# The feed-forward input products, turned: weight columns stand in the array and the tokens move

## The chip, the cores and the metric

The kernel runs on one core of one Trainium2 chip. The metric is the device time of one execution in microseconds. A core has five engines with instruction queues of their own: TensorE (PE, matmuls; PEld is its loading of the operand that stands in the array), VectorE (DVE), ScalarE (ACT), GpSimd (POOL) and SyncE (SP, which here issues DMAs). They wait for one another by semaphores, and each does its instructions in the order of its queue. Matmuls write to PSUM; VectorE and ScalarE read it.

## The reference

A decoder trunk of two residual layers over 256 tokens of 2048 channels, conditioned on a vector c. Layer 0 mixes by a gated recurrence and softmax attention, layer 1 by gated linear attention; each layer ends with a SwiGLU feed-forward network (FFN) of 5632 hidden channels. All numbers are float32.

```
D_MODEL = 2048; SEQ = 256; DEPTH = 2; D_FF = 5632

def swiglu(h, w_in, w_out):
    a, u = jnp.split(h @ w_in, 2, axis=-1)
    return (jax.nn.silu(a) * u) @ w_out

for layer in range(DEPTH):
    mod = silu_c @ mod_w[layer] + mod_b[layer]
    sh1, sc1, g1, sh2, sc2, g2 = jnp.split(mod, 6, axis=-1)
    h = modulate(rms_norm(x, norm_mix_gain[layer]), sh1, sc1)
    y = hgrn2_fox_mixer(h, ...) if layer % 2 == 0 else gla_mixer(h, ...)
    x = x + g1[:, None, :] * y
    h = modulate(rms_norm(x, norm_ffn_gain[layer]), sh2, sc2)
    x = x + g2[:, None, :] * swiglu(h, ffn_w_in[layer], ffn_w_out[layer])
```

`ffn_w_in` has 2048 rows and 11264 columns in each layer: 5632 for `a`, 5632 for `u`.

## The kernel before

All large products are done with split numbers: an operand is rounded to TensorE's float32r (its high part, `hi`), what is left over is the low part (`lo`), and a product is the sum of three matmuls, high by high, high by low and low by high. Activations are split when they are made: a buffer `hT` or `ct` of the pool `hpool` holds [128 channels, 2 parts, 4 k tiles, 256 tokens]. Weights come as float32 and are split on the way.

The products are one long stream. `add` appends a `Product`, 512 columns of a weight matrix by all of its rows, to a list of pieces. A piece is half of a 1 MB transfer, 1024 weight columns per partition: two k tiles of 128 rows by 512 columns. `drive` walks through the pieces. For piece i it issues what the other parts of the network owe at this place (`run_jobs`), splits the pieces up to i + 2 (`split`: ScalarE copies to `hi`, L166, and VectorE subtracts to `lo`, L168), requests the raw weights of some pieces more on SP's queue (`load`, L159), and multiplies (`multiply`). Raw tiles have 3 buffers, `hi` and `lo` 4 each. In `multiply` the activations stand and the weights move: for each k tile and each of two token tiles, three matmuls (L189 to L191) with 512 moving columns, into an accumulator `acc` of [128 tokens, 2 token tiles, 512 columns], two banks of PSUM. The pool `pp` has two such accumulators, `pm` four single banks for all else.

An FFN input product `F{layer}_{n}` has 256 columns of `a` and the 256 of `u` that belong to them; there are 22 in a layer. Its `done_ffn` has ScalarE take the Silu of the first half out of PSUM (L1141), VectorE multiply by the second (L1142), and two pieces later, as a job, `turn`: TensorE transposes the four 128x128 blocks against an identity (L1148), ScalarE copies the high part to a `ct` buffer (L370) and VectorE subtracts for the low part (L371). The 22 products go in four groups (`FFN_GROUPS`); after a group's products, and one more of the next group, come its four output products `G{layer}_{group}_{nb}`, which use the group's `ct` buffers as standing operand.

Between the pieces run the modulation columns: `mod_block` fetches 1 MB of `mod_w` on GpSimd's queue (L103) and VectorE multiplies and sums it (L108). `run_mod` issues them at a rate, `need_mod` issues those that are left of a part when it is wanted: for the FFN's gate in layer 0 that is at product 4 (`begin_row`). The first product of a layer, `F{layer}_0`, comes straight after a norm, and its first four pieces go one token tile after the other (`by_tile`). `narrow_product` (L274) is another form: the weights of the low-rank gate stand, padded to 128 columns, and 256 tokens move.

The instructions of one engine are put in order by a scheduler that uses the order of the code and its own estimate of times.

Of the kernel before, what the change touches and what calls it, by code (L numbers as in the profile page):

```python
# [7 lines left out]
F32 = mybir.dt.float32  # L8
# [3 lines left out]
ALU = mybir.AluOpType  # L12
# [17 lines left out]
# pieces of the products within which the mixers' steps are to be issued  # L30
# [9 lines left out]
# columns of the packed per-partition parameters  # L40
# [10 lines left out]
class Job:  # L51
    """Steps of arithmetic to be issued between the pieces of the streamed products, before a given piece."""
# [6 lines left out]
class Product:  # L59
    def __init__(self, name, w, act, done, before=None, rate=0.0):  # L60
        self.name, self.w, self.act, self.done, self.before, self.rate = name, w, act, done, before, rate
        self.ps = None
        self.first = self.last = False


def build(tc, ctx, a, out):
# [74 lines left out]
    def add(name, w, act, done, before=None, rate=0.0, first=False, last=False):  # L141
        p = Product(name, w, act, done, before, rate)
        p.first, p.last = first, last
        pieces.extend((p, k) for k in range(2 * len(w)))
# [31 lines left out]
    def multiply(i, tiles=(0, 1)):  # L176
        p, k = pieces[i]
        if p.ps is None:
            p.ps = env["pp"].tile([P, 2, 512], F32, tag="pp", name=f"acc_{p.name}")
        hi, lo = splits[i]  # L180
        last = 4 * len(p.w) - 1
        for kk in range(2):
            kt = k * 2 + kk
            w_hi = hi[:, kk * 512:(kk + 1) * 512]
            w_lo = lo[:, kk * 512:(kk + 1) * 512]
            for t in tiles:
                a_hi, a_lo = p.act(kt, t)
                o = p.ps[:, t, :]
                nc.tensor.matmul(o, a_hi, w_hi, start=(kt == 0), stop=False)  # L189
                nc.tensor.matmul(o, a_hi, w_lo, start=False, stop=False)  # L190
                nc.tensor.matmul(o, a_lo, w_hi, start=False, stop=(kt == last))  # L191

# [86 lines left out]
    def rsqrt(dst, ss, n, width, name):  # L279
        """(ss / n + eps) ** -0.5 with one Newton step."""  # L280
        m = small.tile([P, width], F32, tag=f"rs_m{width}", name=f"rsm_{name}")
        u = small.tile([P, width], F32, tag=f"rs_u{width}", name=f"rsu_{name}")
        nc.vector.tensor_scalar(m, ss, 1.0 / n, EPS, ALU.mult, ALU.add)
        nc.scalar.activation(u, m, AF.Ln)
        nc.scalar.activation(dst, u, AF.Exp, scale=-0.5)
        nc.vector.scalar_tensor_tensor(u, dst, -0.5, dst, ALU.mult, ALU.mult)
        nc.vector.tensor_tensor(u, u, m, ALU.mult)
        nc.vector.scalar_tensor_tensor(dst, u, 1.5, dst, ALU.add, ALU.mult)

    def softplus_neg_abs(dst, z):  # L290
        """ln(1 + exp(-|z|))"""
# [39 lines left out]
    def norm_tile(t):  # L331
        """Normalize, modulate, transpose and split one token tile of x."""
# [26 lines left out]
    def ct_pair(key, n):  # L359
        """Pair n of the split, transposed activations called key: two k tiles of a four-tile buffer."""  # L360
# [19 lines left out]
    def gate_line(l, part):  # L380
        """The gate as a line in DRAM."""
# [35 lines left out]
    class Recurrence:  # L417
        """Both token tiles of one head. q, k: [P, tile, d]; lf: [P, tile, 2, d] (split); v: [P, tile, dv]."""
# [63 lines left out]
        def scores(self, t, levels, dst):  # L482
            """dst(n) -> PSUM [P, 64] of level n"""
# [8 lines left out]
        def cross(self, diagonal):  # L492
            """Scores between the token tiles, and with diagonal those of each token with itself."""
# [13 lines left out]
        def pick(self, n, ts, src):  # L507
            """scatter the compact scores of level n; src: [P, len(ts), 64]"""
# [133 lines left out]
    def fox_gates():  # L642
        """-log f, split, [token, head] per token tile; and -F in columns."""
# [207 lines left out]
    def gla_scores(u):  # L851
# [35 lines left out]
    def gla_output(u):  # L887
        """(steps that need v, steps that need the gate too)"""
# [217 lines left out]
    def begin_out(l, src):  # L1106
        """The old x and the gate row take buffers that the mixer's activations leave."""
# [26 lines left out]

    def done_ffn(l, i):
        def done(ps):
            s = env["pool"].tile([P, 2, 256], F32, tag="fs", name=f"fs{l}_{i}")
            if i == FFN_GROUPS[-1][1] - 1:
                silu_then_exp_ln(s, ps[:, :, :256])
            else:  # L1140
                nc.scalar.activation(s, ps[:, :, :256], AF.Silu)  # L1141
            nc.vector.tensor_tensor(s, s, ps[:, :, 256:], ALU.mult)  # L1142

            def turn():
# [4 lines left out]
                gi = [n for n, (b, e) in enumerate(FFN_GROUPS) if b <= i < e][0]  # L1149
# [36 lines left out]
    def now_act(kt, t):  # L1186
        return env["act"](kt, t)
# [4 lines left out]
    def add_ffn(l, rate):  # L1192
        w1, w2 = a["ffn_w_in"], a["ffn_w_out"]
# [89 lines left out]
def _tiles(w, groups):  # L1283
    """w (K, N) and lists of 512 columns -> (chunk, quad, 128, 4 * 512)."""
# [10 lines left out]
def _layout(i):  # L1295
# [35 lines left out]
    groups = [np.concatenate([r(n * 256, n * 256 + 256), DFF + r(n * 256, n * 256 + 256)]) for n in range(DFF // 256)]  # L1331
    arrays["ffn_w_in"] = np.stack([_tiles(i["ffn_w_in"][l], groups) for l in range(2)])
# [22 lines left out]
```

## Time and profile before

| | |
|---|---|
| median of 3 runs | 2524.02 us (2519.18, 2524.24, 2524.02) |
| profiled execution, its own time (the span on the page) | 2515.9 us |
| TensorE busy | 2450.4 us, 11316 matmuls |
| weight loads of TensorE (PEld) | 2025.2 us |
| VectorE busy | 1771.8 us |
| ScalarE busy | 1160.2 us |
| moved by DMA | 647.49 MB, mean 257 GB/s |

The page and the answers of the trace have engines, source lines, tile names, shapes (partitions x elements), counts, busy time and mean time of one instruction, and behind a bar the idle time ahead of them with what ended it. `acc_F` are the accumulators of the FFN's input products, `acc_G` those of its output products, `acc_C` those of layer 1's mixer. In a timeline the first number is the start in us from the span's start, the second how long. A matmul's length there is from its start to its last result; they are pipelined, and the distance of two starts is what one adds to the time.

### The profile page before, as it was taken

What the parts mean: (1) busy time and instruction counts of PE and PEld (TensorE: products, weight loads), DVE (VectorE), ACT (ScalarE), POOL (GpSimd) and SP (SyncE); (2) the same over time, 40 slices, a digit from 0 to 9 for tenths busy, and PEclk for the clock granted to TensorE, in tenths of its full rate; (3) what the DMA queues carried; (4) which work ended last, traced back from release to release, by engine and by line L of the source; (5) the groups of instructions that cost most, each with busy time, mean ns of one, the idle gap of its engine ahead of it and who ended that gap; (6) DMA issues with size and microseconds to landing.
All of it is one profiled execution on the core that took longest, in us unless ns stands there. A gap on an engine that the chain in (4) does not pass through costs nothing.

```text
span 2515.9 us, 28838 instructions
## 1 busy us (share of the span) xinstructions
PE 2450.4 (97%) x11316; PEld 2025.2 (80%) x11316; DVE 1771.8 (70%) x1975; ACT 1160.2 (46%) x1600; POOL 89.4 (4%) x174
## 2 busy tenths in 40 slices
PE   5899999999999999999999999999999999999999
PEld 3678887887888888888888888888788888888887
DVE  6986887877688767766777777777676545554555
ACT  4365555545434444344345545554544344344443
POOL 0000000000000000000000000000000000000000
PEclk9999999999999999999999999999999999999999
DMA  9973767885899878777776566677477555555554
GB/s 379 422 272 140 274 257 292 340 319 216 287 349 357 317 281 293 287 277 293 287 277 226 202 243 233 242 256 283 169 296 254 191 194 184 196 188 186 199 185 149
DMA packets 93850, 647.49 MB, mean 257 GB/s; under 512 B 10417, under 2 KB 10993, under 8 KB 16401
## 3 DMA queue, kind: packets, MB, share of 16 engines
q1 hardware_dynamic: 70290, 476.59, 52.1%
q0 software_dynamic: 23424, 169.07, 18.1%
q8 instruction: 88, 1.44, 0.2%
q14 instruction: 48, 0.39, 0.0%
HBM read 641.39 MB, written 4.23 MB: 257 GB/s over the span
## 4 chain that ended last, share of the span: by engine, by line
PE 92%; DVE 6%; ACT 1%; issue 0%; DMA 0%; SPq 0%; ACTq 0%; DVEq 0%
PE acc_F L191 13%; PE acc_F L190 13%; PE acc_F L189 13%; PE acc_G L189 6%; PE acc_G L191 6%; PE acc_G L190 6%; PE acc_C L191 4%; PE acc_C L189 4%; PE acc_C L190 3%; DVE mod_s L108 3%; PE acc_B L189 2%; PE acc_B L190 2%; PE acc_B L191 2%; PE acc_O L189 2%; PE acc_O L191 2%; PE acc_O L190 2%
## 5 line engine op out<-in xcount | busy, mean ns | idle before, releaser
L168 DVE TENSOR_TENSOR lo<-raw_F,hi 128x1024 fp32r<-128x1024 f32 x352 | 429.4, 1224 | 296.9 <-ACT hi L166 296.8
L166 ACT CAST hi<-raw_F 128x1024 fp32r<-128x1024 f32 x352 | 370.5, 1053 | 478.3 <-PE acc_F L191 430.0
L191 PE MATMUL acc_F<-hi,hT_f 128*128 128x512 f32 x1408 | 551.3, 392 | 1.4 <-DVE hT_f L355 1.4
L189 PE MATMUL acc_F<-hi,hT_f 128*128 128x512 f32 x1408 | 548.4, 390 | 1.8 <-ACT hT_f L354 1.8
L190 PE MATMUL acc_F<-lo,hT_f 128*128 128x512 f32 x1408 | 548.5, 390 | 0.0
L108 DVE SCALAR_TENSOR_TENSOR mod<-mod,silu_c 128x2048 f32<-128x2048 f32 x160 | 365.4, 2285 | 11.1 <-DMA mod<-in_mod_w_dram 11.1
L168 DVE TENSOR_TENSOR lo<-raw_G,hi 128x1024 fp32r<-128x1024 f32 x176 | 214.2, 1222 | 138.3 <-ACT hi L166 138.1
L191 PEld LDWEIGHTS acc_F<-hi,hT_f 128*128 128x128 f32 x1408 | 264.4, 188 | 56.6 <-DVE hT_f L355 3.0
L189 PEld LDWEIGHTS acc_F<-hi,hT_f 128*128 128x128 f32 x1408 | 264.5, 188 | 56.1 <-ACT hT_f L354 2.2
L166 ACT CAST hi<-raw_G 128x1024 fp32r<-128x1024 f32 x176 | 185.4, 1054 | 268.6 <-PE acc_G L191 224.8
L190 PEld LDWEIGHTS acc_F<-lo,hT_f 128*128 128x128 f32 x1408 | 264.3, 188 | 55.2
L189 PE MATMUL acc_G<-hi,ct_f 128*128 128x512 f32 x704 | 273.5, 389 | 1.6 <-DVE res_G L403 1.6
L191 PE MATMUL acc_G<-hi,ct_f 128*128 128x512 f32 x704 | 274.4, 390 | 0.0
L190 PE MATMUL acc_G<-lo,ct_f 128*128 128x512 f32 x704 | 273.8, 389 | 0.0
L168 DVE TENSOR_TENSOR lo<-raw_C,hi 128x1024 fp32r<-128x1024 f32 x96 | 116.8, 1222 | 58.4 <-ACT hi L166 58.0
L189 PEld LDWEIGHTS acc_G<-hi,ct_f 128*128 128x128 f32 x704 | 132.2, 188 | 29.6 <-DVE res_G L403 2.4
L189 PE MATMUL acc_C<-hi,hT_n 128*128 128x512 f32 x384 | 154.3, 402 | 0.9 <-ACT hT_n L354 0.9
L190 PEld LDWEIGHTS acc_G<-lo,ct_f 128*128 128x128 f32 x704 | 132.2, 188 | 27.4
L191 PEld LDWEIGHTS acc_G<-hi,ct_f 128*128 128x128 f32 x704 | 132.2, 188 | 27.2
L191 PE MATMUL acc_C<-hi,hT_n 128*128 128x512 f32 x384 | 150.5, 392 | 0.7 <-DVE hT_n L355 0.7
L190 PE MATMUL acc_C<-lo,hT_n 128*128 128x512 f32 x384 | 150.9, 393 | 0.0
L166 ACT CAST hi<-raw_C 128x1024 fp32r<-128x1024 f32 x96 | 100.7, 1052 | 94.7 <-PE acc_C L191 88.4
(335 smaller groups left out, 3424.0 us busy)
## 6 DMA issues: line engine op xcount, KB each, us to landing
raw_F<-in_ffn_w_in_dram SPq DMA_DIRECT2D x176, 1024.0 KB, 4.9
mod<-in_mod_w_dram POOLq DMA_DIRECT2D x160, 1024.0 KB, 5.2
raw_G<-in_ffn_w_out_dram SPq DMA_DIRECT2D x88, 1024.0 KB, 4.9
raw_C<-in_gla_w_in_dram SPq DMA_DIRECT2D x48, 1024.0 KB, 6.0
mod_s<-in_mod_w_dram SPq DMA_DIRECT2D x32, 1024.0 KB, 10.6
raw_B<-in_ab_w_in_dram SPq DMA_DIRECT2D x32, 1024.0 KB, 5.9
raw_s<-in_start_w_dram SPq DMA_DIRECT2D x16, 1024.0 KB, 8.8
raw_A<-in_ab_w_in_dram SPq DMA_DIRECT2D x16, 1024.0 KB, 5.0
```

The costliest lines, as they stand in the source:

```text
L108: nc.vector.scalar_tensor_tensor(tile, tile, 1.0, silu_c, ALU.mult, ALU.mult, accum_out=modc[l, part][:, j:j + 1])
L166: nc.scalar.copy(out=hi, in_=w)
L168: env["lo"] = nc.vector.tensor_tensor(lo, w, hi, ALU.subtract)
L189: nc.tensor.matmul(o, a_hi, w_hi, start=(kt == 0), stop=False)
L190: nc.tensor.matmul(o, a_hi, w_lo, start=False, stop=False)
L191: nc.tensor.matmul(o, a_lo, w_hi, start=False, stop=(kt == last))
```

## The change

Products 1 to 21 of each layer's FFN are turned: the weight columns stand in the array and the tokens move, so that the result is channel-major and goes to the `ct` buffer without a transpose. Product 0 stays as it was. A turned product comes in two halves, each a `Product` of its own with 128 columns of `a` and their 128 of `u`: 256 columns by 2048 rows, two transfers of 1 MB, 4 pieces. A piece now has four k tiles of 256 columns. Its accumulator has for each of the two 128-column blocks one bank: 256 tokens by the high part of the activations, and 256 by the low part. The high part of the weights is multiplied with both in one matmul of 512 moving columns, the low part with the high part of the activations alone, 256 moving columns, into the first half of the bank. At the end the two halves of the bank are added.

```diff
-    def add(name, w, act, done, before=None, rate=0.0, first=False, last=False):
+    def add(name, w, act, done, before=None, rate=0.0, first=False, last=False, turned=False):
...
         hi, lo = splits[i]
+        if p.turned:
+            multiply_turned(p, k, hi, lo)
+            return
...
+    def multiply_turned(p, k, hi, lo):
+        for kk in range(4):
+            kt = k * 4 + kk
+            both = p.act(kt)
+            for c in range(2):
+                cs = slice(kk * 256 + c * P, kk * 256 + (c + 1) * P)
+                o = p.ps[:, c]
+                nc.tensor.matmul(o, hi[:, cs], both, start=(kt == 0), stop=False, skip_group_check=True)
+                nc.tensor.matmul(o[:, :T], lo[:, cs], both[:, 0], start=False, stop=(kt == KT - 1), skip_group_check=True)
...
-        def act(kt, t):
+        def act(kt, t=None):
             tl = tiles(kt // 4) if callable(tiles) else tiles[kt // 4]
+            if t is None:
+                return tl[:, :, kt % 4, :]
...
+    def done_ffn_turned(l, i, half):
+        def done(ps):
+            s = env["pool"].tile([P, 2, T], F32, tag="fs", name=f"fs{l}_{i}_{half}")
+            nc.scalar.copy(out=s, in_=ps[:, :, T:])
+            nc.vector.tensor_tensor(s, s, ps[:, :, :T], ALU.add)
+            if i == FFN_GROUPS[-1][1] - 1 and half == 1:
+                silu_then_exp_ln(s[:, 0], s[:, 0])
+            else:
+                nc.scalar.activation(s[:, 0], s[:, 0], AF.Silu)
+            nc.vector.tensor_tensor(s[:, 0], s[:, 0], s[:, 1], ALU.mult)
+            gi = group_of(i)
+            c, k0 = ct_pair(f"f{l}{gi}", i - FFN_GROUPS[gi][0])
+            nc.scalar.copy(out=c[:, 0, k0 + half], in_=s[:, 0])
+            nc.vector.tensor_tensor(c[:, 1, k0 + half], s[:, 0], c[:, 0, k0 + half], ALU.subtract)
+        return done
...
-                add(f"F{l}_{n}", quads(w1[l, n]), now_act, done_ffn(l, n), before, rate, n == 0)
+                if n == 0:
+                    add(f"F{l}_{n}", quads(w1[l]), now_act, done_ffn(l, n), before, rate, True)
+                else:
+                    for half in range(2):
+                        m = 2 * n + half - 2
+                        add(f"F{l}_{n}_{half}", [wt[l, m, qd] for qd in range(2)], now_act, done_ffn_turned(l, n, half),
+                            before if half == 0 else None, rate, turned=True)
...
+    w = i["ffn_w_in"].reshape(2, 2, 8, P, 2, DFF // P, P)[:, :, :, :, :, 2:]
+    arrays["ffn_w_turned"] = np.ascontiguousarray(w.transpose(0, 5, 1, 3, 2, 4, 6)).reshape(2, DFF // P - 2, 2, P, 2048)
```

The order of instructions, first on TensorE, in layer 0's product 10, where piece 233 ends and piece 234 begins. `acc_F0_10` is the product's accumulator, `hi_234` and `lo_234` the split weights of piece 234, `hT_f0_1` the second buffer of activations, `fs0_9` the gated result of product 9. Before:

```order
L191 MATMUL acc_F0_10_6857<-hi_233_6822,hT_f0_0_4669 128x512
L189 MATMUL acc_F0_10_6857<-hi_234_6851,hT_f0_1_4670 128x512
L190 MATMUL acc_F0_10_6857<-lo_234_6852,hT_f0_1_4670 128x512
L1148 MATMUL hT_F0_9_6844<-ident_74,fs0_9_6841 128x128 x4
L191 MATMUL acc_F0_10_6857<-hi_234_6851,hT_f0_1_4670 128x512
```

Now, the same piece (in the first half of product 10):

```order
L204 MATMUL acc_F0_10_0_7190<-hT_f0_1_4670,hi_233_7154 128x512
L205 MATMUL acc_F0_10_0_7190<-hT_f0_1_4670,lo_233_7155 128x256
L204 MATMUL acc_F0_10_0_7190<-hT_f0_2_4671,hi_234_7184 128x512
L205 MATMUL acc_F0_10_0_7190<-hT_f0_2_4671,lo_234_7185 128x256
L204 MATMUL acc_F0_10_0_7190<-hT_f0_2_4671,hi_234_7184 128x512
```

Matmuls of 512 and 256 columns take turns, 16 in a piece where 12 of 512 were, and the four transposes of the product ahead are gone.

Next VectorE, at the end of layer 0's FFN input: product 21 is the last, and its result is wanted by the fourth group's output products. `lo_379` to `lo_383` are splits of the output weights (piece 376 is the first of `G0_3_0`, 380 the first of `G0_3_1`), `mod1_3_6` is a modulation column, `ct_f03_1` the buffer that takes the result. Before:

```order
L1142 TENSOR_TENSOR fs0_21_9569<-fs0_21_9569,acc_F0_21_9432 128x512
L168 TENSOR_TENSOR lo_379_9600<-raw_G0_3_0_1_9465,hi_379_9599 128x1024
L168 TENSOR_TENSOR lo_380_9616<-raw_G0_3_1_0_9502,hi_380_9615 128x1024
L168 TENSOR_TENSOR lo_381_9634<-raw_G0_3_1_0_9502,hi_381_9633 128x1024
L108 SCALAR_TENSOR_TENSOR mod1_3_6_9649,modc1_3_91<-mod1_3_6_9649,silu_c_72 128x2048
L371 TENSOR_TENSOR ct_f03_1_9423<-hT_F0_21_9573,ct_f03_1_9423 128x512
```

Now:

```order
L168 TENSOR_TENSOR lo_379_10377<-raw_G0_3_0_1_10213,hi_379_10376 128x1024
L1159 TENSOR_TENSOR fs0_21_1_10349<-fs0_21_1_10349,acc_F0_21_1_10267 128x512
L168 TENSOR_TENSOR lo_380_10393<-raw_G0_3_1_0_10265,hi_380_10392 128x1024
L1164 TENSOR_TENSOR fs0_21_1_10349<-fs0_21_1_10349 128x256
L168 TENSOR_TENSOR lo_381_10411<-raw_G0_3_1_0_10265,hi_381_10410 128x1024
L108 SCALAR_TENSOR_TENSOR mod1_3_6_10426,modc1_3_91<-mod1_3_6_10426,silu_c_72 128x2048
L1168 TENSOR_TENSOR ct_f03_1_10068<-fs0_21_1_10349,ct_f03_1_10068 128x256
```

Three instructions of half 21_1, add, multiply and subtraction, stand between the splits where a multiply and a subtraction stood, and the subtraction still comes last, behind the split of piece 381 and a modulation column. On TensorE the output product that follows begins with piece 376; the first matmul that uses the high part of half 21_1 has 50 matmuls of `G0_3_0` and `G0_3_1` ahead of it, the first that uses the low part 66.

More of the change, by code (lines that the diff above doesn't have):

```diff
@@ L62, in __init__ @@
         self.ps = None
-        self.first = self.last = False
+        self.first = self.last = self.turned = False
 def build(tc, ctx, a, out):
@@ L139, in build @@
     now = [0]
-    def add(name, w, act, done, before=None, rate=0.0, first=False, last=False):
+    def add(name, w, act, done, before=None, rate=0.0, first=False, last=False, turned=False):
         p = Product(name, w, act, done, before, rate)
-        p.first, p.last = first, last
+        p.first, p.last, p.turned = first, last, turned
         pieces.extend((p, k) for k in range(2 * len(w)))
@@ L1137, in done @@
             s = env["pool"].tile([P, 2, 256], F32, tag="fs", name=f"fs{l}_{i}")
[L1138 to L1141, printed above, removed]
+            nc.scalar.activation(s, ps[:, :, :256], AF.Silu)
             nc.vector.tensor_tensor(s, s, ps[:, :, 256:], ALU.mult)
@@ L1148, in turn @@
                         nc.tensor.transpose(pT[:, k * T + t * P:k * T + (t + 1) * P], s[:, t, k * P:(k + 1) * P], ident)
[L1149 removed]
+                gi = group_of(i)
                 split_columns(pT, None, f"f{l}{gi}", i - FFN_GROUPS[gi][0])
@@ L1330, in _layout @@
     arrays["gla_w_out"] = _tiles(i["gla_w_out"][0], nb)
-    groups = [np.concatenate([r(n * 256, n * 256 + 256), DFF + r(n * 256, n * 256 + 256)]) for n in range(DFF // 256)]
-    arrays["ffn_w_in"] = np.stack([_tiles(i["ffn_w_in"][l], groups) for l in range(2)])
+    first = np.concatenate([r(256), DFF + r(256)])
+    arrays["ffn_w_in"] = np.stack([_tiles(i["ffn_w_in"][l], [first])[0] for l in range(2)])
+    w = i["ffn_w_in"].reshape(2, 2, 8, P, 2, DFF // P, P)[:, :, :, :, :, 2:]
+    arrays["ffn_w_turned"] = np.ascontiguousarray(w.transpose(0, 5, 1, 3, 2, 4, 6)).reshape(2, DFF // P - 2, 2, P, 2048)
     arrays["ffn_w_out"] = np.ascontiguousarray(
```

6 lines of the change are left out of this document (4 added, 2 removed).

## The prediction

> **What bounds the kernel now.** I read the page's busy shares and its chain first, to see which engine sets the end.
>
> ```profile
> PE 2450.4 (97%) x11316; PEld 2025.2 (80%) x11316; DVE 1771.8 (70%) x1975; ACT 1160.2 (46%) x1600; POOL 89.4 (4%) x174
> ...
> PE 92%; DVE 6%; ACT 1%; issue 0%; DMA 0%; SPq 0%; ACTq 0%; DVEq 0%
> ```
>
> TensorE is it. Since its busy time is partly modelled, I then asked whether it also runs without gaps in the stretch that is edited: the waits of TensorE over the whole span (us in total, times, longest), and two stretches of six FFN input products each, one of either layer, from the busy time by stretch (after the length come busy time and instructions of PE, PEld, DVE, ACT and POOL, then the granted clock, the DMAs' share and GB/s).
>
> ```profile
> PE acc_F L189 <- ACT hT_f L354: 1.8, 2, 0.9
> PE acc_F L191 <- DVE hT_f L355: 1.4, 2, 0.7
> ```
>
> ```profile
> 834.38:967.33 132.95, 132.95 (x598) 110.10 (x597) 94.68 (x87) 55.44 (x58) 6.76 (x13) 1.00 0.80 286
> 2002.10:2135.04 132.94, 132.94 (x597) 110.09 (x596) 67.52 (x60) 55.43 (x58) 0.00 (x0) 1.00 0.55 190
> ```
>
> On all input products together TensorE waits 3.2 us, all of it for the norm at their start; the clock is granted in full; and both stretches last the same 132.9 us though VectorE and the DMAs carry different loads. So in this stage the time is the number of matmuls times their spacing. Everything below is about spacings, taken from starts in the timeline and not from the "mean ns", which is a latency: 390 ns matmuls start every 227 ns. First and last of 54 like matmuls (53 steps):
>
> ```profile
> 799.70 0.39 PE L189 MATMUL acc_G<-hi,ct_f 128*128 128x512 f32 x1
> ...
> 811.71 0.39 PE L191 MATMUL acc_G<-hi,ct_f 128*128 128x512 f32 x1
> ```
>
> 12.01 us / 53 = 226.6 ns for 512 moving columns, each with a weight load of its own.
>
> **The matmuls.** A piece (1024 weight columns) took 12 matmuls of 512 columns. Turned, it has eight 128x128 blocks of the high part, each against 512 columns (256 tokens of both activation parts), and eight of the low part, each against 256. That is 6144 streamed columns either way, but 16 weight loads and starts in place of 12. What decides is the spacing of a 256-column matmul. The trace has 32 of them in a row, also with a fresh 128x128 load each, inside the low-rank gate's product:
>
> ```profile
> 1376.06 0.39 PE L190 MATMUL acc_C<-lo,hT_n 128*128 128x512 f32 x1
> 1376.29 3.95 PE L274 MATMUL nacc_glow<-hT_n,nw_glow 128*128 128x256 f32 x32
> 1380.08 0.40 PE L191 MATMUL acc_C<-hi,hT_n 128*128 128x512 f32 x1
> ```
>
> ```profile
> 1376.07 3.97 PEld L274 LDWEIGHTS nacc_glow<-hT_n,nw_glow 128*128 128x128 f32 x32
> ```
>
> From 1376.29 to 1380.08 are 32 steps: 118.4 ns each, and the 512-column one ahead keeps its 0.23 us. Half of 226.6 would be 113.3, so a 256-column matmul costs 5.1 ns more than half of a 512-column one. Turned, a piece takes 8 x (226.6 + 118.4) = 2760 ns instead of 12 x 226.6 = 2719.2: 40.8 ns more. Product 0 of each layer stays as it was; 21 products x 8 pieces x 2 layers = 336 pieces make **+13.7 us** on TensorE, all of it on the path, since there are no gaps to take it up. The bounds: not below 113.3 (+0), as the streamed columns alone are half, and not above the load's own 188 ns (row of the weight loads below), which would be +201 us; I take 118.4, the same shape and engine. What the trace doesn't have is the alternation 512, 256, 512; the step from 512 into 256 and that from 256 into 512, both in the fence, show no surcharge. Nor does it have a moving operand of two runs of 256 a few KB apart; I cost that at nothing, since bytes and columns are the same, and keep some chance for it.
>
> ```profile
> L189 PEld LDWEIGHTS acc_F<-hi,hT_f 128*128 128x128 f32 x1408 | 264.5, 188 | 56.1 <-ACT hT_f L354 2.2
> ```
>
> A rule speaks against the change. The load at 1376.07 begins while the matmul of 1376.06 streams, so here loads run under matmuls that use all rows. The Trainium skill, "TensorE: Matmul & The Clock Gate", Part 3 ("What overlaps and what doesn't"), says that a weight load overlaps matmuls in flight only where the row groups differ, and its section on LDWEIGHTS prices one at columns / 1.2 ns, 107 ns here. By that rule the 4 added loads of each piece would be bare: 4 x 336 x 107 ns = 144 us slower, as an estimate from that page. The trace disagrees: matmuls that each bring a load of 188 ns stand 226.6 and 118.4 ns apart.
>
> **The transposes.** Each product ended with four 128x128 transposes on TensorE. One turn:
>
> ```profile
> 1060.75 0.60 PE L1148 MATMUL hT_F<-ident,fs 128*128 128x128 f32 x4
> 1061.11 0.47 PE L191 MATMUL acc_F<-hi,hT_f 128*128 128x512 f32 x1
> 1061.42 0.39 PE L189 MATMUL acc_F<-hi,hT_f 128*128 128x512 f32 x1
> ```
>
> 0.36 us until the next product matmul starts, and that one needs 0.31 instead of 0.23: 0.45. The stretch 2002.10:2135.04 says it whole: 576 product matmuls x 226.6 = 130.5 us; the remaining 2.4 us over its 5 turns (20 transposes in x597) is 0.48 each. 42 turns go (one per layer stays): 42 x 0.475 = **-19.9 us**, on the path too. Bounds 0.45 to 0.48: -18.9 to -20.2.
>
> **Evacuation, on ScalarE and VectorE.** Per product before: Silu of 512 from PSUM, multiply, and after the turn a copy and a subtraction of 512. Now, per half product: copy 512 out of PSUM, add 512, Silu, multiply, copy and subtract at 256 each.
>
> ```profile
> L1142 DVE TENSOR_TENSOR fs<-fs,acc_F 128x512 f32<-128x512 f32 x44 | 30.2, 687 | 26.7 <-ACT fs L1141 25.1 <-ACT fs L297 1.4
> L371 DVE TENSOR_TENSOR ct_f<-hT_F,ct_f 128x512 fp32r<-128x512 f32 x44 | 30.0, 685 | 1.5 <-ACT ct_f L370 1.4
> L983 DVE TENSOR_TENSOR hT_s<-tm_s,hT_s 128x256 fp32r<-128x256 f32 x16 | 6.7, 419 | 12.0 <-ACT hT_s L982 12.0
> L370 ACT CAST ct_f<-hT_F 128x512 fp32r<-128x512 f32 x44 | 25.5, 581 | 3.1 <-PE hT_F L1148 3.1
> L1141 ACT ACTIVATE fs<-acc_F 128x512 f32<-128x512 f32 x42 | 25.1, 598 | 65.8 <-PE acc_F L191 65.8
> L982 ACT CAST hT_s<-tm_s 128x256 fp32r<-128x256 f32 x16 | 6.5, 405 | 0.5
> ```
>
> VectorE: 0.687 + 0.685 = 1.37 us a product before, 2 x (0.69 + 0.42 + 0.42) = 3.06 after: +1.7 us in 22. ScalarE: 0.598 + 0.581 = 1.18 before, 2 x (0.58 + 0.405 + 0.405) = 2.8 after: +1.6, from 42% to 49% of the stage. Both lie beside TensorE, and the cover is thin at one place only, where layer 0's remaining modulation columns are pressed into products 4 to 6:
>
> ```profile
> 696.00:718.00 22.00, 22.00 (x99) 18.23 (x98) 19.18 (x18) 8.92 (x9) 2.11 (x4) 1.00 0.88 341
> 718.00:740.00 22.00, 22.00 (x99) 18.23 (x98) 18.61 (x18) 8.93 (x9) 2.11 (x4) 1.00 0.94 356
> 740.00:762.00 22.00, 22.00 (x105) 18.27 (x104) 17.78 (x17) 10.17 (x13) 1.59 (x3) 1.00 0.96 362
> 762.00:784.00 22.00, 22.00 (x100) 18.21 (x99) 18.43 (x19) 9.77 (x11) 1.58 (x3) 1.00 0.98 397
> ```
>
> VectorE is busy 74.0 of these 88 us. Four products add 6.8: 80.8, 92%. Its weight splits run ahead of TensorE: a piece's buffers (four) come free three pieces before it is needed, 8.2 us, and the two splits take 2.3 (1.05 and 1.22, rows below), so VectorE may be 5.9 us late before TensorE sees it. I cost this at 0. Bounds: -0, as no wait is removed, and +6.8, if every added microsecond came through.
>
> The new waits: a half product's accumulator must be drained before the next but one starts. Its copy and add end some 3 us after its last matmul; the other half takes 11 us. And the last product's result is wanted soon, by the last group's first output product. Take the last matmul of half 21_1 as zero. ScalarE makes a split (to 1.05), the copy (1.65), a split that waits for a piece at 2.72 (3.8), the Silu, a table load, a split that waits for 5.44 (6.5), and the high part (6.9). VectorE makes a split (2.3), the add (3.0), a split (5.0), the multiply (5.4), a split (7.7), a modulation column (10.0) and the low part (10.4).
>
> ```profile
> L166 ACT CAST hi<-raw_F 128x1024 fp32r<-128x1024 f32 x352 | 370.5, 1053 | 478.3 <-PE acc_F L191 430.0
> L168 DVE TENSOR_TENSOR lo<-raw_F,hi 128x1024 fp32r<-128x1024 f32 x352 | 429.4, 1224 | 296.9 <-ACT hi L166 296.8
> L108 DVE SCALAR_TENSOR_TENSOR mod<-mod,silu_c 128x2048 f32<-128x2048 f32 x160 | 365.4, 2285 | 11.1 <-DMA mod<-in_mod_w_dram 11.1
> ```
>
> ```profile
> 1298.87 1.28 ACT L299 ACT_TABLE_LOAD   x1
> ```
>
> In the new order the matmul that needs the high part stands behind 50 others of 226.6 ns (11.3 us), that for the low part behind 66 (15.0). Both have over 4 us to spare: 0. The input weights still come in 176 transfers of 1 MB on SP's queue, in the same places of it, and POOL's queue is untouched: 0.
>
> ```profile
> raw_F<-in_ffn_w_in_dram SPq DMA_DIRECT2D x176, 1024.0 KB, 4.9
> ```
>
> **The sum.** 2515.9 + 13.7 - 19.9 = 2509.7 in the profiled execution, whose own time is its span. The median of the runs, 2524.0, lies 8.1 above that span; the 8.1 stays, so **2517.8, said as 2518 us**. Of this kernel a measurement tells about 0.2%, 5 us, from no change.
>
> **Rivals.** Three ways it could go otherwise:
> - The short matmul hides its successor's load less well in the alternation (this one ends on the other side). The sum breaks even at a spacing of 113.3 + 19.9 us / 2688 = 120.7 ns, only 2.3 above my row, and reads slower by 0.2% from 122.6. At the load's own 188 ns it would be 2518 + 2688 x 69.6 ns = 2705. For it: single steps in the run of 32 must scatter about the mean. Against: that mean holds over 32 loads. 8%, most of it near 125 ns, 2536. The Trainium skill's rule above ("TensorE: Matmul & The Clock Gate", Part 3) is the same rival at its far end.
> - Nothing to measure: 120 ns (2522) instead of 118.4, or up to 6.8 us of late splits in products 4 to 6 (2525). For it: the two terms are of like size and opposite sign. 28%.
> - More gain: 113.3 ns, the columns alone, gives 2524.0 - 19.9 = 2504. For it: the load has finished under the long matmul, so only one of two steps is tight. 8%.
>
> **How the numbers follow.** My forecast, a gain of 5 to 15 us (2509 to 2519 is its own range), gets 46%. Slower by over 0.2% gets 18%: 8% by the loads, 6% by VectorE in the pressed stretch, should its in-order waits on ScalarE add to the 6.8 us, and 4% by the two-run moving operand, at which 5 ns on each of 2688 long matmuls is 13 us. Faster: 46 + 8 = 54%; same 28%. The range for 8 in 10 reaches from 2504, the columns alone, to 2533, which takes in break-even, the 6.8 us and short matmuls to 124 ns.
>
> **What would show it.** Right: 48 turned pieces in 48 x 2.76 = 132.5 us where 132.94 stood, no TensorE wait on input products beyond the norm's, no L1148 group but 8 transposes, VectorE near 92% at 696 to 784. Wrong: short matmuls more than 121 ns apart, long ones off 226.6, or TensorE idle before input products behind a split, an add or a high part.

## The result, and the profile after

The changed kernel takes 2534.8 us (median of 4 runs, 2531.5 to 2535.7) where the kernel before takes 2521.9 in the runs beside it: ratio 1.0052, 95% interval 1.0038 to 1.0066. It is slower by half a per cent, where 2518 us and a gain were forecast; the time lies 2 us above the range.

The page of the changed kernel, busy time of each engine and the chain's shares:

```profile
PE 2469.4 (97%) x12492; PEld 2078.0 (82%) x12492; DVE 1825.2 (72%) x2143; ACT 1211.2 (48%) x1768; POOL 89.4 (4%) x174
...
PE 92%; DVE 6%; ACT 1%; issue 0%; DMA 0%; SPq 0%; ACTq 0%; DVEq 0%
```

TensorE is the bound as before, with 19 us more of busy time. The waits of TensorE on FFN input products (us in total, times, longest):

```profile
PE acc_F L192 <- ACT hT_f L370: 1.8, 2, 0.9
PE acc_F L194 <- DVE hT_f L371: 1.4, 2, 0.7
```

Only the norm at the start of either layer is waited for, with the same microseconds as before: no new wait came. So the loss is in the spacing of the matmuls. The stretch of six input products of layer 1 that stood at 132.94 us, now from the first product matmul to the first of the output products (the instructions of the accumulators alone: length, then busy time and count on PE, PEld, DVE and ACT, clock, DMA share, GB/s):

```profile
2014.52:2150.19 135.67, 135.67 (x768) 117.47 (x767) 7.49 (x11) 6.37 (x11) 1.00 0.52 187
```

135.67 us for 384 pairs of a long and a short matmul: 353.3 ns a pair, where 345.0 were forecast. Against before it is 2.72 us more. Before's stretch holds five of its six turns; the sixth falls into the output products behind it, which take 65.29 us now and took 65.78. That leaves 2.2 us per six products, some 16 us for the 42 turned ones if all were like these, where the medians differ by 12.9. The two profiled spans differ by 18.0 (2533.9 and 2515.9), but not all of it is the change. Product 0 of layer 1, which the edit leaves alone, before and now:

```profile
1776.12:1802.85 26.73, 26.04 (x129) 21.54 (x129) 19.43 (x35) 18.37 (x33) 0.00 (x0) 1.00 0.41 142
```

```profile
1786.63:1814.95 28.32, 27.63 (x129) 22.67 (x129) 19.47 (x35) 18.41 (x33) 0.00 (x0) 0.94 0.38 135
```

In the changed kernel's profiled execution the granted clock is 0.50 for 3.4 us of this product (1789.0 to 1792.4), and likewise in layer 0's product 0 (from 611.4) and ahead of it (from 553.4). That makes 1.6, 1.6 and 1.3 us which before's profiled execution doesn't have; without them the spans differ by 13.5. Which of the two steps grew, from starts in the timeline:

```profile
2030.05 0.40 PE L204 MATMUL acc_F<-hT_f,hi 128*128 128x512 f32 x1
2030.29 0.28 PE L205 MATMUL acc_F<-hT_f,lo 128*128 128x256 f32 x1
2030.41 0.40 PE L204 MATMUL acc_F<-hT_f,hi 128*128 128x512 f32 x1
2030.65 0.28 PE L205 MATMUL acc_F<-hT_f,lo 128*128 128x256 f32 x1
2030.76 0.40 PE L204 MATMUL acc_F<-hT_f,hi 128*128 128x512 f32 x1
2030.99 0.28 PE L205 MATMUL acc_F<-hT_f,lo 128*128 128x256 f32 x1
2031.11 0.40 PE L204 MATMUL acc_F<-hT_f,hi 128*128 128x512 f32 x1
```

Long to short 0.24, 0.24 and 0.23 us, short to long 0.12, 0.11 and 0.12: the short step is about what was forecast (117 ns in the trace), and the long one is some 9 ns over its 226.6, which the prediction had named as a sign of its being wrong.

VectorE in the pressed stretch (696 to 784 us) has 78.3 of 88 us, 89%, and the new evacuation costs what the nearest rows said:

```profile
sum 88.00, PE 88.00 PEld 76.06 DVE 78.27 ACT 41.76 POOL 7.40; mean PE 22.00 PEld 19.01 DVE 19.57 ACT 10.44 POOL 1.85
```

```profile
L1159 DVE TENSOR_TENSOR fs<-fs,acc_F 128x512 f32<-128x512 f32 x84 | 57.2, 681 | 0.6 <-ACT fs L1158 0.6
L1158 ACT COPY fs<-acc_F 128x512 f32<-128x512 f32 x84 | 48.6, 579 | 1.9 <-PE acc_F L205 1.9
```

### The profile page after: what moved, and what is told of

Its sections match the earlier page's. It is cut to its first block, busy times and chain, and to the rows that moved or that the text cites. A ratio compares the mean times of both kernels' runs of the same rounds, so it can differ in the third digit from the quotient of the medians.

```text
span 2533.9 us, 31800 instructions
## 1 busy us (share of the span) xinstructions
PE 2469.4 (97%) x12492; PEld 2078.0 (82%) x12492; DVE 1825.2 (72%) x2143; ACT 1211.2 (48%) x1768; POOL 89.4 (4%) x174
## 4 chain that ended last, share of the span: by engine, by line
PE 92%; DVE 6%; ACT 1%; issue 0%; DMA 0%; SPq 0%; ACTq 0%; DVEq 0%
PE acc_F L204 25%; PE acc_F L205 13%; PE acc_G L192 6%; PE acc_G L194 6%; PE acc_G L193 6%; PE acc_C L194 3%; PE acc_C L192 3%; PE acc_C L193 3%; DVE mod_s L108 3%; PE acc_B L192 2%; PE acc_B L194 2%; PE acc_B L193 2%; PE acc_O L192 2%; PE acc_O L193 2%; PE acc_O L194 2%; DVE lo_s L168 1%
## 5 line engine op out<-in xcount | busy, mean ns | idle before, releaser
L204 PE MATMUL acc_F<-hT_f,hi 128*128 128x512 f32 x2688 | 948.1, 398 | 0.0
L205 PE MATMUL acc_F<-hT_f,lo 128*128 128x256 f32 x2688 | 753.9, 280 | 0.0
L204 PEld LDWEIGHTS acc_F<-hT_f,hi 128*128 128x128 f32 x2688 | 504.9, 188 | 124.6
L205 PEld LDWEIGHTS acc_F<-hT_f,lo 128*128 128x128 f32 x2688 | 507.4, 189 | 0.6
L103 POOL DMA_DIRECT2D mod<-in_mod_w_dram x160 | 84.7, 530 | 1683.2 <-DVE mod L108 1542.2
L166 ACT CAST hi<-raw_O 128x1024 fp32r<-128x1024 f32 x64 | 67.4, 1054 | 80.9 <-PE acc_O L194 72.1
```

The costliest lines, as they stand in the source:

```text
L103: nc.gpsimd.dma_start(out=tile, in_=a["mod_w"][l, part * KT + j])
L166: nc.scalar.copy(out=hi, in_=w)
L204: nc.tensor.matmul(o, hi[:, cs], both, start=(kt == 0), stop=False, skip_group_check=True)
L205: nc.tensor.matmul(o[:, :T], lo[:, cs], both[:, 0], start=False, stop=(kt == KT - 1), skip_group_check=True)
```

## The experiments

For most kernels the same row is shown: the second group of six input products in layer 1, accumulators alone, to the first output product. "A pair" is that length divided by 384, the number of pairs in it.

### The layout or the order

Two theories for the long step: its moving operand consists of two runs of 256 that lie 4 KB apart (1), or the lengths alternate (2). The first edit lays both parts side by side; all users of the buffers follow.

```
-        return hpool.tile([P, 2, 4, T], F32R, tag="h", name=name)
+        return hpool.tile([P, 4, 2, T], F32R, tag="h", name=name)
...
-                return tl[:, :, kt % 4, :]
+                return tl[:, kt % 4].rearrange("p s t -> p (s t)")
```

> The changed kernel, with the high and low parts of a k tile's tokens laid side by side in SBUF, so that the 512 moving columns are one run; everything else, the order of the matmuls too, as it was. In the changed kernel a 512-column matmul takes 235.8 ns to the next start and a 256-column one 116.8, where 226.6 and 118.4 were forecast. Theory 1 (the moving operand of two runs costs the 9.2 ns): the long step goes back to 226.6, 2688 x 9.2 ns = 24.7 us less, about 2510 us. Theory 2 (the alternation of long and short matmuls costs it, whatever the layout): no change, 2535 us, long step 236.

```profile
2013.96:2149.63 135.67, 135.67 (x768) 117.71 (x767) 7.49 (x11) 6.39 (x11) 1.00 0.53 187
```

2531.2 us, ratio to before 1.0036 (1.0022 to 1.0050). The stretch is the changed kernel's to the hundredth of a microsecond: theory 1 falls, and with it the only doubt about the operand that the prediction named. The 3.6 us between the two medians aren't in it; three of these five runs had a granted clock of 0.998 or more, three of the changed kernel's four had 0.996.

The second edit orders each piece: eight long matmuls, then eight short ones.

```
+        for part in range(2):
+            for kk in range(4):
...
+                    if part == 0:
+                        nc.tensor.matmul(o, hi[:, cs], both, start=(kt == 0), ...)
+                    else:
+                        nc.tensor.matmul(o[:, :T], lo[:, cs], both[:, 0], ..., stop=(kt == KT - 1), ...)
```

> The changed kernel with the layout of two runs kept, but in each piece the eight 512-column matmuls first and then the eight 256-column ones, so that the alternation is gone but for one step of each kind per piece. Theory 1 (two runs cost): no gain, the long step stays at 236 inside the row of eight, about 2535 us (2539 if short ones in a row take 118.4 instead of 116.8). Theory 2 (the alternation costs): long 226.6 and short 118.4 in their rows, 345.0 a pair for 352.6, 2688 x 7.6 ns = 20 us less, about 2514 us.

```profile
2008.75:2142.80 134.05, 134.05 (x768) 118.05 (x767) 7.49 (x11) 6.38 (x11) 1.00 0.54 192
```

2523.8 us, 1.0008 (1.0000 to 1.0017): 11 us of the expected 20 came back, 349.1 ns a pair. Theory 2 holds in part. Where the rest went is seen in the timeline of this kernel, a row of short ones, a row of long ones and the next short one:

```profile
2021.85 1.00 PE L208 MATMUL acc_F<-hT_f,lo 128*128 128x256 f32 x7
2022.69 2.00 PE L206 MATMUL acc_F<-hT_f,hi 128*128 128x512 f32 x8
2024.53 0.28 PE L208 MATMUL acc_F<-hT_f,lo 128*128 128x256 f32 x1
```

From 2021.85 to 2022.69 seven short steps, 120.0 ns each and not 118.4; from 2022.69 to 2024.53 eight long ones, 230.0 and not 226.6. In the trace the first five long steps are near 234, 236, 228, 232 and 231 ns, the last three 227: 28 ns over in all, of which the first short step behind the row, 114 ns, gives 6 back.

Both edits together:

> Both edits: parts side by side and the matmuls of one length in a row. Theory 1: 345.0 a pair, 2510 to 2514 us, no better than the layout alone. Theory 2: the same 2514 us as the order alone. If each costs a part of the 9.2 ns, this one is faster than either edit alone by several us.

2524.6 us, 1.0009 (1.0000 to 1.0017). The layout adds nothing to the order.

### No long matmuls at all

```
-                nc.tensor.matmul(o, hi[:, cs], both, start=(kt == 0), stop=False, ...)
+                for part in range(2):
+                    nc.tensor.matmul(o[:, part * T:(part + 1) * T], hi[:, cs], both[:, part],
+                                     start=(kt == 0), stop=False, ...)
```

> The changed kernel with each 512-column matmul of two runs made as two 256-column matmuls of one run each, with a weight load for each: no two-run operand, no alternation, 24 matmuls a piece for 16. Both theories price it at 24 x 118.4 = 2842 ns a piece against the 2821 measured for the changed kernel: 336 x 21 ns = 7 us more, about 2542 us. Theory 1 makes more of it: 2 x 118.4 = 236.8 is what the two-run matmul takes, so that a run costs as much as a matmul of its own. If 256-column matmuls take 113.3 in such a row, it is 336 x 102 ns = 34 us faster, 2501 us.

The result of this kernel is not the full product; its instructions and lengths are those of the full computation.

```profile
2029.10:2167.33 138.23, 138.23 (x1152) 138.18 (x1151) 7.49 (x11) 6.39 (x11) 1.00 0.54 184
```

138.23 us / 1152 = 120.0 ns. 2551.6 us, 1.0118 (1.0104 to 1.0131): ten more than expected, because a 256-column matmul in a long row takes 120.0. The row of 32 in the trace of before, whose mean I took, was not such a row: its steps range from 113 to 131 ns.

### Fewer changes of length

```
-        for part in range(2):
+        for part in ((0, 1) if k % 2 == 0 else (1, 0)):
```

> The kernel with eight long and then eight short matmuls per piece, but every second piece begins with its short ones, so that rows of one length are sixteen long and half as many rows of long matmuls follow a row of short ones. In the ordered kernel the first five or so long steps after short ones are 233, 236, 228, 232 and 231 ns and only then 227: some 25 ns for each such change, 336 of them. Theory 2 in this form (the change of length costs, and a long row recovers): half of that goes, 168 x 25 ns = 4 us less than the ordered kernel's 2523.8, about 2520 us, and slow first steps only where short ones stand ahead. Rival: the slow steps belong to the beginning of a piece (new weight tiles, their semaphores), not to the length: then every piece keeps them, 2524 us, and they stand at the beginning of each piece in a row of sixteen.

```profile
2005.97:2139.57 133.60, 133.60 (x768) 117.92 (x767) 7.58 (x11) 6.46 (x11) 1.00 0.53 190
```

2521.0 us, 1.0000 (0.9991 to 1.0009): 347.9 ns a pair. The line through 226.6 and 120.0 ns gives 346.6 for a pair. The ordered kernel is 2.5 over it, 20 ns for its one change per eight pairs; this one 1.3 over it, 21 ns per sixteen. In these two the cost goes with the number of changes, as theory 2 says, and the rival (the beginning of a piece) falls. This is the best turned version that was run, and no faster than the kernel before.

### The transposes alone

In the kernel before, the four transposes of a turn are left out:

```
             def turn():
-                pT = ps_mix(f"hT_F{l}_{i}")
-                for k in range(2):
-                    for t in range(2):
-                        nc.tensor.transpose(...)
...
-                split_columns(pT, None, ...)
+                split_columns(s.rearrange("p t c -> p (t c)"), None, ...)
```

> The kernel before, whose FFN input products are untouched, without the four transposes that end each of them: the split reads the gated result as it lies, so the operand of the output products holds it untransposed (that part is left out). It prices the removed transposes alone. The prediction's 0.475 us a turn, 44 turns here: 20.9 us less than before, about 2501 us. Rival: a turn's time is partly taken back, since the stretch also lasts as long as its weights or splits come: 5 to 10 us less, 2512 to 2517 us.

```profile
1994.79:2125.35 130.56, 130.56 (x576) 107.96 (x575) 3.44 (x5) 2.99 (x5) 1.00 0.55 193
```

2503.2 us, 0.9924 (0.9911 to 0.9938), 18 us less than before's 2521.0 beside it. 132.94 - 130.56 = 2.38 us for five turns, 0.476 each: the forecast's term to the nanosecond. The runs give 18 us and not 20.9; in this kernel's profiled execution product 0 of either layer has 3.4 us at a granted clock of 0.50, as the changed kernel's has. Without these, 1.6 us each, its two FFNs are 20.9 us shorter than before's, and nothing of the term is taken back.

### What the loads and the lengths do

A row of 128-column matmuls, in the ordered kernel:

```
-                        nc.tensor.matmul(o[:, :T], lo[:, cs], both[:, 0], ...)
+                        nc.tensor.matmul(o[:, :P], lo[:, cs], both[:, 0, :P], ...)
```

> The kernel with eight long and then eight short matmuls per piece, with the short ones cut from 256 to 128 moving columns (the low weights' part of half the tokens is left out). It asks why a row of 256-column matmuls settles at 120.0 ns, where half of 226.6 is 113.3. Theory a (a fixed part per matmul: 226.6 and 120.0 for 512 and 256 give 13.4 ns + 0.4164 ns a column): 66.7 ns a step, 2688 x 52.3 ns = 141 us less than the profile of the ordered kernel. Theory b (120.0 is what the weight load of each matmul takes, and columns no longer count): the steps stay near 120 and the time near 2524 us.

```profile
2023.29 0.84 PE L208 MATMUL acc_F<-hT_f,lo 128*128 128x128 f32 x6
2023.97 0.68 PE L206 MATMUL acc_F<-hT_f,hi 128*128 128x512 f32 x2
```

Six steps in 0.68 us, 113 ns each; one run, 2508.2 us. In a row, 128 columns aren't cheaper than some 112 ns, so a floor that the columns don't set lies just under the 120 ns of 256 columns. Theory a fails below 256; theory b has the floor right and puts it 7 ns too high. The first of the eight short steps, right behind a long matmul, is an exception with 58 ns in the trace, and the long step behind the row takes 284. The load is still not bare. The Trainium skill, "TensorE: Matmul & The Clock Gate", Part 3 ("What overlaps and what doesn't"), lets loads overlap only where row groups differ; with the 107 ns of that page's section on LDWEIGHTS for a load, bare, plus 53 ns of columns (128 x 0.416) a step would be 160 by estimate, and the trace disagrees with 113.

Equal lengths, in the changed kernel's order:

```
-                nc.tensor.matmul(o[:, :T], lo[:, cs], both[:, 0], ...)
+                nc.tensor.matmul(o, lo[:, cs], both, ...)
```

> The changed kernel, order and layout as they were, with the low weights' matmul also over 512 columns (it adds the product of the two low parts, which the reference's accuracy doesn't need): each matmul is as long as the one ahead. Theory 2 (the change of length costs): all steps 226.6 ns, 453.2 a pair against 352.6 measured, 2688 x 100.6 ns = 270 us more, about 2804 us. Rival (it is the alternation of high and low weight tiles, or adding to the columns of the accumulator just written, whatever the length): long steps of 236, 2688 x 2 x 9.2 ns = 50 us more than that, 2854 us, or 2829 if only every second step has it.

```profile
2186.13:2360.20 174.07, 174.07 (x768) 144.02 (x767) 7.48 (x11) 6.39 (x11) 1.00 0.41 148
```

2803.3 us (one run), 226.7 ns a step: neither the turns of high and low weights nor the adding to columns just written costs anything. Only with unequal lengths is there a surcharge.

Is it a load that a short stream doesn't cover? The long matmuls' blocks at half width, then the short ones':

```
+                n = P if kt == 0 else 64
+                nc.tensor.matmul(o[:n], hi[:, cs][:, :n], both, ...)
```

> The changed kernel, order and layout as they were, with the weight block of the long matmuls cut from 128 to 64 columns but at the first k tile (half of the high weights' part is left out): the load that must come under a 256-column matmul is half as long, the streams are the same. Theory 2a (a 256-column stream of 113 ns doesn't cover the load of the next block, which sets the step in the row of 128-column matmuls at 112 ns, and the long step after it pays): 226.6 + 113.3 = 339.9 ns a pair for 352.6, 15/16 x 2688 x 12.7 ns = 32 us less, about 2503 us. Theory 2b (a change of length disturbs the stream itself, the loads have no part in it): 352.6 still, 2535 us.

```
+                nc.tensor.matmul(o[:64, :T], lo[:, cs][:, :64], both[:, 0], ...)
```

> The control to the run with halved long blocks: here the weight block of the short matmuls is cut to 64 columns (half of the low weights' part is left out). That load has a 512-column stream over it. Theory 2a: covered before and now, no change, 352.6 ns a pair, 2535 us. Theory 2b: no change either. A gain here would say that a load slows the stream that it runs under, whether or not it is done in time.

```profile
1992.75:2123.76 131.01, 131.01 (x768) 115.92 (x767) 7.47 (x11) 6.37 (x11) 1.00 0.54 194
```

```profile
2001.01:2134.12 133.11, 133.11 (x768) 97.67 (x767) 7.47 (x11) 6.40 (x11) 1.00 0.53 191
```

The first: 341.2 ns a pair, 2502.3 us, as theory 2a says. The control moves too: 346.6 ns, 2515.9 us, which neither theory has; a load that had a 512-column stream over it was not free in this order. The expectations that follow speak of a theory 3: a matmul takes its columns (213.3 ns for 512) and a fixed part of 13.3 ns, half of it for half a weight block, and an alternation 6.7 ns a pair beside them. Its forms 3a and 3b differ in when that surcharge is paid. Next, short matmuls of 320, 384 and 448 columns (parts side by side, so that the operand is one run; n is the number):

```
+                nc.tensor.matmul(o[:, :n], lo[:, cs], both[:, :n], ...)
```

> The changed kernel with both parts of a k tile side by side, and the low weights' matmul over 320 columns in place of 256 (it adds the product of both low parts for 64 of the tokens). A stream of 320 columns lasts 320 x 0.4426 = 141.6 ns, longer than any load. Theory 2a: both loads are covered, 226.6 + 141.6 = 368.2 ns a pair for 352.6, 2688 x 15.6 ns = 42 us more, about 2577 us by the 2534.8 of the changed kernel. Theory 2b: the long step keeps its 235.8 and the time is 2602 us.

> The same with 384 columns (the low parts' product for 128 of the tokens). Theory 3 gives 213.3 + 160 + 26.7 = 400.0 ns a pair, the short step 173.3, under the 188 ns of a load. 3a and 3b: both keep the surcharge here, 406.7 ns, 2688 x 54.1 = 145 us over the changed kernel, about 2680 us. Without it: 2662 us.

> As the run with 320 columns for the low weights' matmul, but 448 (both low parts' product is added for 192 of the tokens). Theory 3 gives 213.3 + 186.7 + 2 x 13.3 = 426.7 ns a pair, the short step 200.0. 3a (the surcharge is there while a load's 188 ns don't fit into the step they run in): no surcharge, 426.7 ns, 2688 x 74.1 = 199 us over the changed kernel, about 2734 us. 3b (any change of length costs it): 433.4 ns, 2752 us.

```profile
2064.85:2210.74 145.89, 145.89 (x768) 130.01 (x767) 7.48 (x11) 6.39 (x11) 1.00 0.49 175
```

```profile
2111.43:2267.58 156.15, 156.15 (x768) 139.13 (x767) 7.49 (x11) 6.40 (x11) 1.00 0.46 165
```

```profile
2158.10:2326.20 168.10, 168.10 (x768) 143.99 (x767) 7.49 (x11) 6.36 (x11) 1.00 0.42 153
```

379.9, 406.6 and 437.8 ns a pair (2611.7, 2683.8 and 2760.4 us, one run each). A longer short step doesn't help: 2a and 3a fall. The line (0.4164 ns a column and 13.4 ns a matmul) gives 373.2, 399.9 and 426.6, so the pairs lie 6.7, 6.7 and 11.2 over it, and the changed kernel's own pair, 353.3 against 346.6, also 6.7.

These are prices of one stretch, and the surcharge isn't paid everywhere. Products 2 to 4 of the changed kernel, in layer 0 and in layer 1:

```profile
660.96:728.80 67.84, 67.84 (x386) 58.86 (x385) 4.08 (x6) 3.48 (x6) 1.00 0.83 313
1837.66:1904.23 66.57, 66.57 (x387) 58.20 (x386) 4.09 (x6) 3.47 (x6) 1.00 0.79 304
```

For 192 pairs (the counts take in the matmuls at the edges) that is 353.3 and 346.7 ns: the same matmuls at the same clock, and in layer 1 the alternation runs on the line, without a surcharge. In the trace it does so from the four transposes of product 0 (1819.88) until a single matmul with a weight block of 16 columns comes between (L403, 1923.16); from there on it is 353.3 again. In layer 0 the same two places leave it at 353.3 and then take it down to 346.7. In these products the control with halved short blocks gives 346.7 and 340.0 (layers 0 and 1), 384 columns 413.3 in both, 448 columns 437.8 and 433.3; 320 columns and the halved long blocks give what they give above. The stretches above begin alike, behind output products, and so can be compared. But the 6.7 ns that the control gained are as much as lies between the two states, and what puts the stream into one or the other no run tested.

The fixed part by the size of the block, with all lengths 512: both matmuls at n = 64.

```
+                nc.tensor.matmul(o[:n], hi[:, cs][:, :n], both, ...)
+                nc.tensor.matmul(o[:n], lo[:, cs][:, :n], both, ...)
```

> The kernel in which both matmuls of a pair have 512 columns, with all weight blocks but the first k tile's cut to 64 columns (half of the FFN input's channels are left out). No alternation, loads of half size with 512 columns over them. Theory 3: 213.3 + 6.7 = 220.0 ns a step in place of 226.6, 15/16 x 5376 x 6.7 ns = 34 us less than the 2803 of the same kernel with full blocks, about 2770 us. Rival (a load that is covered costs nothing, the step is columns only): 226.6 still, 2803 us.

```profile
2196.28:2372.76 176.48, 176.48 (x768) 105.41 (x767) 7.49 (x11) 6.35 (x11) 1.00 0.41 146
```

2819.4 us, 229.8 ns a step: half the load made it slower, so theory 3's fixed part doesn't belong to the block's size. Last, rows of one length that isn't 512 (n is 512 at the first k tile):

```
+                nc.tensor.matmul(o[:, :n], hi[:, cs], both[:, :n], ...)
+                nc.tensor.matmul(o[:, :n], lo[:, cs], both[:, :n], ...)
```

> The changed kernel with the parts side by side and both matmuls of a pair over 448 columns, but at the first k tile, where both have 512 (the low part of 64 tokens is left out of the high weights' product, and some of both low parts' product is added). No change of length within 15 of 16 pairs. Theory 4 (the change of length costs): 448 x 0.4426 = 198.3 ns a step, 396.6 a pair. Theory 5 (any length but 512 costs about 6 ns a matmul, as 256 does in a row): 204 ns, 408 to 410 a pair. In time, with 453.2 for each sixteenth pair: 2535 + 127 = 2662 us against 2692 us.

> The same with 384 columns for both (the low part of 128 of the tokens is left out). Theory 4: 170.0 ns a step, 340 a pair, about 2519 us. Theory 5: 175.7, the value that the short step of 384 has in the alternation, 351.4 a pair, about 2548 us.

```profile
2111.66:2268.46 156.80, 156.80 (x768) 144.04 (x767) 7.47 (x11) 6.36 (x11) 1.00 0.46 165
```

```profile
2015.14:2151.07 135.93, 135.93 (x768) 133.70 (x767) 7.47 (x11) 6.31 (x11) 1.00 0.52 186
```

Less 24 pairs of 453.3 ns, the other 360 take 405.3 and 347.4 ns: steps of 202.7 and 173.7, 2685.6 and 2537.1 us. Theory 4 falls, since 448 and 384 exceed the columns' share without any change of length; theory 5 is 1 to 2 ns a step too high. What it took for a price of every length but 512 is mostly the fixed part: the line gives 200.0 and 173.3. Away from the 512-column pairs the steps of 384 are 173.3 in the trace, on the line; those of 448 go from 199 to 207 and stay 2.7 over it, for which no run here gives a reason. What a change of length costs comes on top.

## Why the prediction was wrong, point by point

**The matmuls: the step that failed.** The prediction took the pair of the alternation as the sum of two spacings measured in rows of one length, 345.0 ns. The term was 336 x (8 x (226.6 + 118.4) - 2719.2) = +13.7 us. By the same count the 353.3 ns give 336 x (8 x 353.3 - 2719.2) = +36.0, 22.3 more. The miss has two parts, 2688 pairs each:
- 1.6 ns, 4.3 us: a short matmul in a row is 120.0, not 118.4. The row of 32 that I divided is not steady (113 to 131 ns), and its mean hid that. From 226.6 and 120.0 every matmul has a fixed part of 13.4 ns beside 0.4164 ns a column (384 columns: 173.3 on the line, 173.7 measured; 448: 200.0 and 202.7). The Trainium skill, "TensorE: Matmul & The Clock Gate", section "Back-to-back issue gap", has this form, columns / 2.4 + 2.5 ns, for the gap of single matmuls without the loads of a stream; the slope agrees (0.4164 against 0.4167), the fixed part here, with a load for each matmul, is five times as large.
- 6.7 ns, 18.0 us: the alternation. I named it as not in the trace and excluded a surcharge by the two steps at the ends of the row of 32: the 512-column one ahead of it, 0.23 us, and the last 256-column one. The step that grew is another, the long one behind a short one. It begins at 1380.08, and the fence ends there. Further along the same timeline of before stood these:

```profile
1381.46 0.39 PE L191 MATMUL acc_C<-hi,hT_n 128*128 128x512 f32 x1
...
1382.82 0.39 PE L191 MATMUL acc_C<-hi,hT_n 128*128 128x512 f32 x1
```

From the start at 1380.08 to 1381.46 are six steps of 230.0 ns (1.387 us in the trace's nanoseconds, 231 a step), to 1382.82 six more of 226.7. The six after the short row cost some 27 ns more, like the long rows of the ordered kernel. That a long step behind a short one is dearer could have been read there, over six steps and not over one in units of 10 ns. What an alternation makes of it couldn't: 6.7 ns a pair in most of it, nothing in some 330 pairs (products 1 to 5 of layer 1 above all), which take 2.2 us off the 36.0.

**The rivals.** The one that ends slower was right in the number (125 ns for the short step, 2536 us; counted that way the short step is 353.3 - 226.6 = 126.7) and got 8%. Its mechanism, a short stream over a load, is only half supported: half blocks for the long matmuls take the surcharge away, but streams of 320 and 384 columns keep all of it, and products 2 to 4 of layer 1 go without it with loads and streams as they are. The 4% for the two-run operand had the right place, the long matmul, and the wrong cause; with the parts side by side nothing is gained. My case against the first, "that mean holds over 32 loads", was true of a row and said nothing of an alternation.

**The transposes.** -19.9 us: right, 0.476 us a turn where 0.475 was used.

**Evacuation and waits.** Right at 0: no added wait of TensorE, VectorE at 89% of the pressed stretch where 92% was forecast, 0.68 and 0.58 us for the add and the copy where 0.69 and 0.58 were used. The last group's high and low parts are waited for nowhere.

**The base.** The 8.1 us between the profiled span and the median were scatter of before's runs, not a part that stays: the changed kernel's median lies 0.9 above its span, and before's own median is 2521.9 and 2521.0 in the later runs. This hid 2 us of the miss: the time came out 17 us above 2517.8, the change (12.9 where -6.2 was forecast) 19 us. With the right pair the steps give 2509.7 + 22.3 - 2.2 = 2529.8, or 13.9 us more than before's span; the half clock's 4.4 make it 2534.2, and the span is 2533.9.

## What to carry over

A matmul's price was a line here, not a share of its columns: more and shorter matmuls pay the fixed part again (here 13.4 ns, 18 us for 16 in place of 12), so a rearrangement that keeps the streamed columns still has to be paid for by what it removes. Don't alternate lengths; put equal ones in rows as long as the buffers allow, which here was worth 14 us (2534.8 to 2521.0). And where an edit makes a pattern that the trace lacks, look for its elements over several steps, since a single step in rounded units hides the few nanoseconds that a count of 2688 turns into the result.

## What was not expected of the hardware

- After a change from short to long matmuls some five 512-column steps take 228 to 236 ns until they settle at 227, about 28 ns in all, or 20 with the shorter first step of the next short row. In an alternation of 512 with 256, 320 or 384 columns the pair pays 6.7 ns in the stretch shown.
- The same alternation of 512 and 256 columns runs at 353.3 or at 346.7 ns a pair in one execution, over hundreds of pairs, and goes from one to the other where a few other matmuls come between.
- With 128x128 blocks a row of 128-column matmuls runs at 113 ns a step, hardly under the 120 of 256 columns: in a row, little is to be gained below 256 columns.
- Half a weight block speeds up the alternation (353.3 to 341.2 or 346.6 ns a pair) and slows down a row of 512 (226.7 to 229.8 a step, single ones from 0.224 to 0.236 us). Loads and streams may disturb each other in a way that depends on their phase, which would fit the two states above; that reading is argued. What in the engine makes it so stays open, and no theory above gives all of these numbers.
